# Attention projections on one core: the split weights of the first token half are kept in DRAM and read back for the second

## The chip, the core and the metric

The kernel runs on one core of a Trainium2 chip. A core has five engines with a queue of instructions each: TensorE (PE in the profile; its weight loads are shown apart as PEld), VectorE (DVE), ScalarE (ACT), GpSimd (POOL) and SyncE (SP), which in this kernel mostly issues DMA transfers. Engines run side by side and wait for each other by semaphores; transfers between DRAM and on-chip memory run on the core's 16 DMA engines. The metric is the time on the device in microseconds (us) of one execution, as the median over several.

## The reference

Two residual layers over 1024 tokens of width 1024, in float32, and a last RMSNorm. Layer 0 has a retention and RWKV-7 mixer; layer 1, which the change touches, has grouped-query attention over a window of 128 tokens with a learned sink per head. A SwiGLU FFN follows each.

```python
def swa_sink_mixer(h, w_qkv, b_qkv, sinks, w_o, b_o):
    z = h @ w_qkv + b_qkv
    q, k, v = jnp.split(z, [SWA_WIDTH, SWA_WIDTH + SWA_KV_HEADS * HEAD_DIM], axis=-1)
    ...
    s = jnp.einsum('bnqhgd,bnkhd->bnhgqk', q, kb).astype(jnp.float32) * HEAD_DIM ** -0.5
    s = jnp.where(valid[None, :, None, None], s, -jnp.inf)
    m = jnp.maximum(jnp.max(s, axis=-1, keepdims=True), sink)
    e = jnp.exp(s - m)
    p = e / (jnp.sum(e, axis=-1, keepdims=True) + jnp.exp(sink - m))
    o = jnp.einsum('bnhgqk,bnkhd->bnqhgd', p.astype(vb.dtype), vb)
    return o.reshape(B, T, SWA_WIDTH) @ w_o + b_o

def reference(x, ...):
    h = x
    for layer in range(DEPTH):
        n = rms_norm(h, norm1_g[layer])
        h = h + (retention_rwkv_mixer(n, ...) if layer % 2 == 0 else swa_sink_mixer(n, ...))
        n = rms_norm(h, norm2_g[layer])
        h = h + swiglu(n, ffn_w_gate[layer], ffn_w_up[layer], ffn_w_down[layer])
    return rms_norm(h, final_g)
```

w_qkv is 1024 x 1536 (16 query heads, 4 key heads and 4 value heads of 64), w_o is 1024 x 1024.

## The kernel before

Features lie on the 128 partitions and tokens along the free axis. The 1024 tokens are worked in two halves of 512 (`hf` 0 and 1), and each half runs through every weight, so each weight of the attention is loaded twice.

**Splitting.** Matrix products are made from operands split in two: a high part rounded to the type fp32r and a low part, which is what the rounding leaves. A product is three matmuls, high by high, high by low and low by high (`gemm`, L350 to L352). For a weight the split runs on the chip. `wraw` (L303) loads 128 columns of a weight, 128 x 1024 raw numbers or 512 KB, from DRAM through SP's queue (L305) into one of two buffers `wr`. `wsplit` (L327) cuts it into two tiles of 512 columns: for each, ACT casts the high part (L335) and an engine named by `self.lo` subtracts (L336) to give the low part. In the attention that engine is DVE. A split tile of 128 x 2 x 512 numbers is 512 KB. `wtile` (L317) hands out its place: in the attention and the FFN around it, from a ring of six, four under the tag `w` and two under `wx`. One weight is two tiles, and one `gemm` with it is 24 matmuls of 128 x 128 by 128 x 512.

**Keeping.** The mixer of layer 0 already stores its split weights in DRAM in token half 0 (`wsplit` with `keep`, L338) and reads them back in half 1 (`wkept`, L308, the transfer at L313, from a ring of four), under the name `wsp`.

**The attention.** `attn(hf)` makes 12 projections with `proj`: two tiles of keys, two of values, eight of queries; each loads a weight, runs a gemm and scales the result on DVE and on ACT. The keys are copied with halves exchanged to a second tile `ks` by two DMAs each on SP's queue (L1520, L1521). Then for each of four groups of heads, after its two query projections, four blocks of 128 queries: scores on PE (L1552), the mask added on DVE (L1556), the row maximum on DVE (L1562), the exponentials on ACT (L1569), the scaling by the sum on DVE (L1578) and for one head of four on ACT, transposes on PE (L1585), the product with the values on PE (L1595), and the split of the result (L1601 on ACT, L1602 on DVE). These are 16 blocks in each half, 32 in all. `w_o(hf)` then runs eight more weights over the result and adds it to the residual (L1613).

**The order.** In `trunk` the calls stand as: norm of half 0, two of the eight output tiles of the down projection of layer 0's FFN for half 1 (`rest_d`), `attn(0)`, the rest of those, norm of half 1, `w_o(0)`, `form0` (it forms the operands of the next FFN for half 0 and stores them in DRAM as `bd`, by eight DMAs at L1134), `attn(1)`, five pairs of the first part of the FFN of layer 1 (`early`), `w_o(1)`, and the rest of the FFN. That is only the order in which they are written down: when the kernel is built, a scheduler with a model of time fills each engine's queue from all of them, as far as buffers and data allow, so gemms of one part run between the softmax steps of another. On the chip each queue then runs in the order that was built.

Of the kernel before, what the change touches and what calls it, by code (L numbers as in the profile page):

```python
# [10 lines left out]
F32 = mybir.dt.float32  # L11
# [5 lines left out]
P = 128  # L17
T = 1024
HT = 512
# [85 lines left out]
class Plan:  # L105
# [3 lines left out]
    def __init__(self, K):  # L109
        self.K, self.now, self.ev, self.banks = K, 0.0, {}, []  # L110
        self.gens, self.jobs, self.cur, self.twice = [], deque(), None, ()
# [93 lines left out]
class Kern:  # L205
    def __init__(self, ctx, tc, A, out):
        self.ctx, self.tc, self.nc, self.A, self.out = ctx, tc, tc.nc, A, out
        nc = self.nc
        self.pp = ctx.enter_context(tc.tile_pool(name="pp", bufs=1, side="left"))
        self.dr = ctx.enter_context(tc.tile_pool(name="dr", bufs=2, space=bass.MemoryType.DRAM))  # L210
        self.n = 0
        pad = ctx.enter_context(tc.tile_pool(name="pad", bufs=1, side="right"))
        pt = pad.tile([P, 120], F32, tag="pad", name="pad")
        nc.gpsimd.memset(pt, 0.0)
        nc.scalar.activation(pt[:, :16], pt[:, :16], AF.Copy)
        self.gapt(self.pp, 32)
        self.pv = self.t(self.pp, [P, NPV], "pv")
        nc.scalar.dma_start(self.pv, A["pvec"])
        self.cst = {}
        for nm in ("ones", "eps"):  # L220
            self.cst[nm] = self.const(self.pp, nm)
        self.h, self.plan = [None, None], None
        self.wx = None
        self.w6, self.nw, self.owed, self.lo = False, 0, [], self.nc.gpsimd
        self.hid = [self.dram(f"hid{i}", [FT, P, HT]) for i in range(4)]
        self.hc = [self.dram(f"hc{L}", [NP, 4, P, 2, HT]) for L in range(2)]
        self.bd = self.dram("bd", [KT, P, HT])
        self.u0d = self.dram("u0", [NP, 2, P, HT])
        self.wsp = self.dr.tile([30, 2, P, 2, HT], F32, tag="wsp", name="wsp", bufs=1)
        self.cats = [self.dram(f"cat{hf}", [KT, P, HT]) for hf in range(2)]  # L230

    def psum(self, name, bufs):
# [109 lines left out]
    def wload(self, ap, width=1024):  # L342

        return self.wsplit(self.wraw(ap, width), width)

    def gemm(self, ps, w, rhs):
        nc = self.nc
        n = len(rhs)
        for k, ((hi, lo), (rh, rl)) in enumerate(zip(w, rhs)):
            nc.tensor.matmul(ps, hi, rh, start=k == 0, stop=False)  # L350
            nc.tensor.matmul(ps, hi, rl, start=False, stop=False)  # L351
            nc.tensor.matmul(ps, lo, rh, start=False, stop=k == n - 1)  # L352
# [1145 lines left out]
    def attn(self, hf, nr, ap, n8):  # L1498
# [4 lines left out]
        amask, sink, b8 = self.amask, self.sink, self.b8  # L1503

        def proj(ti, out, **kw):
            w = self.wload(self.A["w_qkv"][ti])
            ps = self.pst("f", [P, HT])
            self.gemm(ps, w, nT)
            V.tensor_tensor(out=out, in0=ps, in1=r, op=ALU.mult)
            S.activation(out, out, AF.Identity, **kw)  # L1510

        kc, ks = [], []
        for i in range(2):
            kt = self.t(ap, [P, P + HT], f"kc{i}", 2)
            proj(8 + i, kt[:, P:], bias=self.col("bqkv", 8 + i))
            st = self.t(ap, [P, P + HT], f"ks{i}", 1)
            lo = 0 if hf else P
            if hf:
                G.tensor_copy(kt[:, 0:P], self.pk[i][:, HT : HT + P])
            nc.sync.dma_start(st[0:64, lo:], kt[64:128, lo:])  # L1520
            nc.sync.dma_start(st[64:128, lo:], kt[0:64, lo:])  # L1521
            kc.append(kt)
            ks.append(st)
# [4 lines left out]
        for i, vc in enumerate(vcs):  # L1528
            proj(10 + i, vc, bias=self.col("bqkv", 10 + i))
# [8 lines left out]
        for g in range(4):  # L1538
            for i in (2 * g, 2 * g + 1):
                proj(i, qt[i], scale=0.125, bias=b8[:, i : i + 1])  # L1540
            for b in range(4):
                ti, rg = g // 2, g % 2
# [62 lines left out]
    def w_o(self, hf, ch):  # L1605
        nc = self.nc
        h = self.h[hf]
        for d in range(KT):
            w = self.wload(self.A["w_o"][d])
            ps = self.pst("f", [P, HT])  # L1610
            self.gemm(ps, w, ch)
            hk = self.kt(h)(d)
            nc.vector.scalar_tensor_tensor(  # L1613
                out=hk, in0=hk, scalar=self.col("bo", d), in1=ps, op0=ALU.add, op1=ALU.add
            )
# [225 lines left out]
```

## Time and profile before

| | us |
|---|---|
| three runs | 2384.56, 2380.51, 2376.88 |
| their median | 2380.51 |
| the profiled execution | 2374.81 |
| its span in the trace | 2373.0 |

In the profile, a row "L335 ACT CAST w<-wr" is an instruction of line 335 on ACT that reads `wr` and writes `w`. A matmul reads a moving operand and a weight (`ps_f<-n,w`). Half 0 of the attention runs in about 1310 to 1515 us of the trace, half 1 in about 1515 to 1760, each with parts of the neighbouring stages between. Matmuls overlap, so that one of 0.39 us may start 0.23 us after the one before.

### The profile page before, as it was taken

The numbers are of one execution on the slowest core, as the hardware profiler recorded it, in microseconds if no ns is written. First come the engines' busy times: TensorE is split into PE (matmuls) and PEld (weight loads), VectorE is DVE, ScalarE is ACT, GpSimd is POOL, SyncE is SP. The second block draws the span as 40 slices with busy tenths as digits, with TensorE's granted clock in tenths as the row PEclk, the third lists the DMA queues.
The fourth block names the chain that finished last, engine by engine and source line by source line (L and its number), as shares of the span: only waits on it lengthen the run. The fifth ranks groups of instructions, "written<-read, shape, count | busy, mean of one in ns | idle before, by whom it ended". The sixth has DMA issues, their size and how long they took to land. (4 is left out here: it accounts for less than half of the span.)

```text
span 2373.0 us, 35626 instructions
## 1 busy us (share of the span) xinstructions
PE 2312.1 (97%) x13092; PEld 1828.9 (77%) x13092; DVE 1667.4 (70%) x2630; ACT 1054.7 (44%) x1946; POOL 948.4 (40%) x746
## 2 busy tenths in 40 slices
PE   8999999999999999999999999999999999999997
PEld 6777777777777888888778877777787888877885
DVE  6876865774667358887675668567548778888776
ACT  5354533324456333333333556557645333333335
POOL 3123221201342057776667300002103577767665
PEclk9999999999999999999999999999999999999998
DMA  7555544443445545554554321232236465547652
GB/s 271 203 199 197 176 154 132 128 115 114 148 164 183 208 164 206 211 197 163 218 220 142 123 66 64 71 127 71 100 128 221 170 216 213 209 175 280 245 193 87
DMA packets 167741, 395.92 MB, mean 167 GB/s; under 512 B 42896, under 2 KB 45584, under 8 KB 167568
## 3 DMA queue, kind: packets, MB, share of 16 engines
q1 hardware_dynamic: 164448, 388.15, 47.8%
q10 hardware_dynamic: 2832, 4.45, 0.5%
q8 instruction: 104, 1.70, 0.3%
q0 software_dynamic: 288, 1.05, 0.1%
q14 instruction: 69, 0.57, 0.1%
HBM read 271.29 MB, written 116.92 MB: 164 GB/s over the span
## 5 line engine op out<-in xcount | busy, mean ns | idle before, releaser
L240 PE MATMUL ps_f<-n,w 128*128 128x512 f32 x1440 | 385.6, 415 | 8.6 <-ACT w L335 6.4
L240 PEld LDWEIGHTS ps_f<-n,w 128*128 128x128 f32 x1440 | 268.2, 192 | 93.6 <-issue 24.5
L335 ACT CAST w<-wr 128x512 fp32r<-128x512 f32 x244 | 147.9, 612 | 182.9 <-PE ps_f L352 73.1
L336 POOL TENSOR_TENSOR w<-wr,w 128x512 fp32r<-128x512 f32 x68 | 92.1, 1363 | 280.0 <-ACT w L335 223.0
L336 DVE TENSOR_TENSOR w<-wr,w 128x512 fp32r<-128x512 f32 (+1 forms) x176 | 123.8, 706 | 71.5 <-ACT w L335 71.3
L336 POOL TENSOR_TENSOR w<-wq,w 128x512 fp32r<-128x512 f32 x92 | 130.5, 1431 | 29.2 <-ACT w L335 27.2
L351 PE MATMUL ps_f<-n,w 128*128 128x512 f32 x356 | 141.7, 398 | 0.0
L352 PE MATMUL ps_f<-n,w 128*128 128x512 f32 x356 | 141.0, 396 | 0.6 <-POOL w L336 0.6
L350 PE MATMUL ps_f<-n,w 128*128 128x512 f32 x356 | 140.8, 396 | 0.6 <-ACT n L1601 0.5
L1182 DVE TENSOR_TENSOR nq<-ps_m,u 128x512 f32<-128x512 f32 x88 | 58.8, 685 | 104.3 <-PE ps_m L1177 104.2
L336 POOL TENSOR_TENSOR wx<-wr,wx 128x512 fp32r<-128x512 f32 x8 | 10.6, 1319 | 301.8 <-ACT wx L335 301.6
L1175 PE MATMUL ps_f<-n,w 128*128 128x512 f32 x298 | 118.5, 398 | 4.7 <-DVE h L1375 3.1
L1175 PE MATMUL ps_m<-n,w 128*128 128x512 f32 x300 | 117.5, 392 | 1.5 <-DVE h L1375 1.5
L1176 PE MATMUL ps_f<-n,w 128*128 128x512 f32 x298 | 117.2, 393 | 0.1
L1176 PE MATMUL ps_m<-n,w 128*128 128x512 f32 x300 | 116.8, 389 | 0.0
L1177 PE MATMUL ps_m<-n,w 128*128 128x512 f32 x300 | 116.8, 389 | 0.0
L1177 PE MATMUL ps_f<-n,w 128*128 128x512 f32 x298 | 116.7, 393 | 0.0
L358 POOL TENSOR_TENSOR n<-nq,n 128x512 fp32r<-128x512 f32 x54 | 91.5, 1707 | 8.9 <-ACT n L356 8.9
L1175 PE MATMUL ps_m<-cb,w 128*128 128x512 f32 x240 | 93.4, 389 | 1.0 <-DVE nq L1182 1.0
L1176 PE MATMUL ps_m<-cb,w 128*128 128x512 f32 x240 | 93.4, 389 | 0.0
L1177 PE MATMUL ps_m<-cb,w 128*128 128x512 f32 x240 | 93.4, 389 | 0.0
L1349 POOL TENSOR_TENSOR w<-wd,w 128x512 fp32r<-128x512 f32 (+1 forms) x53 | 76.0, 1444 | 34.8 <-ACT w L1348 34.8
(525 smaller groups left out, 6467.1 us busy)
## 6 DMA issues: line engine op xcount, KB each, us to landing
hc<-n SPq DMA_DIRECT2D x74, 512.0 KB, 2.6
wsp<-w SPq DMA_DIRECT2D x54, 512.0 KB, 3.3
w<-wsp SPq DMA_DIRECT2D x54, 512.0 KB, 3.4
wq<-in_w_gate SPq DMA_DIRECT2D x44, 512.0 KB, 4.3
u<-u SPq DMA_DIRECT2D x88, 256.0 KB, 2.9
n<-hc SPq DMA_DIRECT2D x43, 512.0 KB, 5.5
wr<-in_w_in SPq DMA_DIRECT2D x34, 512.0 KB, 4.8
hid<-n SPq DMA_DIRECT2D x66, 256.0 KB, 2.0
```

What stands on the lines that cost most here:

```text
L240: self.nc.tensor.matmul(out, lhsT, rhs, **kw)
L335: nc.scalar.copy(hi[:, :n], raw[:, c])
L336: self.lo.tensor_tensor(out=lo[:, :n], in0=raw[:, c], in1=hi.bitcast(F32)[:, :n], op=ALU.subtract)
L350: nc.tensor.matmul(ps, hi, rh, start=k == 0, stop=False)
L351: nc.tensor.matmul(ps, hi, rl, start=False, stop=False)
L352: nc.tensor.matmul(ps, lo, rh, start=False, stop=k == n - 1)
L358: e.tensor_tensor(out=lo, in0=src, in1=hi.bitcast(F32), op=ALU.subtract)
L1175: mm(ps, hi, xh, start=first and k == 0, stop=False, skip_group_check=True)
L1176: mm(ps, hi, xl, start=False, stop=False, skip_group_check=True)
L1177: mm(ps, lo, xh, start=False, stop=last and k == len(w) - 1, skip_group_check=True)
L1182: add = lambda o, x, y: V.tensor_tensor(out=o, in0=x, in1=y, op=ALU.add)
L1349: nc.gpsimd.tensor_tensor(out=lo, in0=v, in1=hi.bitcast(F32), op=ALU.subtract)
```

## The change

A tile `wsa` is added in DRAM for the 20 weights of the attention (12 of w_qkv, 8 of w_o), in two split tiles each. A new method `wtwice` takes the place of `wload` at both calls. In half 0 it loads and splits as before and stores each split tile to `wsa`; in half 1 it reads the two tiles back into the ring, and does not load the raw weight or split it. All of these transfers are on SP's queue. One line is added at L230 and eleven behind `wload`, so that the line numbers of the changed kernel are higher by 1 from there and by 12 from `gemm` on.

```diff
         self.wsp = self.dr.tile([30, 2, P, 2, HT], F32, tag="wsp", name="wsp", bufs=1)
+        self.wsa = self.dr.tile([20, 2, P, 2, HT], F32, tag="wsa", name="wsa", bufs=1)
...
+    def wtwice(self, ap, kept, again):
+
+        if not again:
+            return self.wsplit(self.wraw(ap), keep=kept)
+        res = []
+        for i in range(2):
+            w = self.wtile()
+            self.nc.sync.dma_start(w.bitcast(F32), kept[i])
+            res += [(w[:, 0, k * P : k * P + P], w[:, 1, k * P : k * P + P]) for k in range(4)]
+        return res
...
         def proj(ti, out, **kw):
-            w = self.wload(self.A["w_qkv"][ti])
+            w = self.wtwice(self.A["w_qkv"][ti], self.wsa[ti], hf)
...
         for d in range(KT):
-            w = self.wload(self.A["w_o"][d])
+            w = self.wtwice(self.A["w_o"][d], self.wsa[12 + d], hf)
```

## The prediction

> **What bounds the kernel now.** I read the busy shares first, then the waits of TensorE (PE) around the two attention layers, then the stretches in which the edited lines run. The first row is from the page, the rows under it from the table of stretches (its columns: stretch, length, then busy time and instruction count of PE, of its weight loads, of VectorE (DVE), ScalarE (ACT) and GpSimd (POOL), granted clock, DMA share, GB/s), and the last three from the list of PE's waits between 1300 and 1800 us (total, times, longest).
>
> ```profile
> PE 2312.1 (97%) x13092; PEld 1828.9 (77%) x13092; DVE 1667.4 (70%) x2630; ACT 1054.7 (44%) x1946; POOL 948.4 (40%) x746
> ```
>
> ```profile
> 1310.00:1515.00 205.00, 200.77 (x1014) 152.96 (x1013) 146.67 (x324) 121.92 (x307) 18.84 (x18) 1.00 0.23 75
> 1515.00:1760.00 245.00, 245.00 (x1198) 186.23 (x1197) 152.75 (x308) 138.07 (x320) 31.11 (x24) 1.00 0.30 99
> ```
>
> ```profile
> PE ps_y L1595 <- DVE n L1602: 2.1, 3, 0.9
> PE ps_m L1585 <- DVE s L1578: 1.7, 1, 1.7
> PE ps_f L350 <- ACT n L1601: 0.5, 1, 0.5
> ```
>
> Attention of token half 0 lies in the first stretch, that of half 1 in the second. In the second PE is busy 245.00 of 245.00 us at full clock, while DVE has 92 us and ACT 107 us free: nothing that those engines do holds PE up. All of PE's waits in the region are 4.3 us; that is 205.00 − 200.77 = 4.2 of the first stretch, so all lie in half 0, none in half 1. The two lines that split a weight, L335 and L336, release none of them.
>
> **The change part by part.** Half 1 loses 20 raw loads, 40 casts on ACT and 40 subtractions on DVE, and gains 40 reloads; half 0 gains 40 stores. The built order of each engine confirms it: ACT falls by 40 instructions, DVE by 40, SP rises by 60 DMA issues, and PE and POOL keep their counts.
>
> *Removed work.* The groups by line in 1515 to 1760 (count | busy, mean ns | idle time before, and what ended it):
>
> ```profile
> L335 ACT CAST w<-wr 128x512 fp32r<-128x512 f32 x46 | 28.4, 618 | 42.5 <-PE ps_f L352 36.7 <-PE ps_f L1177 5.1 <-DMA wr<-in_w_qkv 0.5
> L335 ACT CAST wx<-wr 128x512 fp32r<-128x512 f32 x22 | 13.7, 620 | 20.8 <-PE ps_f L352 18.2 <-DMA wr<-in_w_qkv 2.6
> L336 DVE TENSOR_TENSOR w<-wr,w 128x512 fp32r<-128x512 f32 x29 | 20.0, 689 | 20.3 <-ACT w L335 20.2
> ```
>
> 40 × 0.618 = 24.7 us go from ACT and 40 × 0.689 = 27.6 us from DVE. The casts stand waiting for PE (36.7 and 18.2 us for a gemm to free a tile), not PE for them. So the saving lands on engines that already wait for PE, in a stretch where PE has no idle time to give back: 0 us. Between the ends 0 and −27.6, PE's 245.00 of 245.00 says 0. The Trainium skill, page "Perfetto Trace Analysis", section "Identifying the Most-Contended Engine", holds that matmul busy time is a bad measure of how full TensorE is, because matmuls are pipelined, and that the busy share of weight loads is a good one: by it this term could be larger than 27.6 us, which is Rival C's second price.
>
> *Reloads in half 1.* A reload is one 512 KB transfer into one ring tile. It may start once PE has finished with the tile that held the slot, and must land before PE comes to it. PE in time order, where the ring of six runs with nothing between:
>
> ```profile
> 1517.05 0.39 PE L350 MATMUL ps_f<-n,wx 128*128 128x512 f32 x1
> ...
> 1519.77 0.39 PE L350 MATMUL ps_f<-n,wx 128*128 128x512 f32 x1
> ...
> 1533.37 0.39 PE L350 MATMUL ps_f<-n,wx 128*128 128x512 f32 x1
> ```
>
> The tile of 1517.05 is done with by 1519.77, 2.72 us for 12 matmuls, 0.227 us each; its slot's next content is first read at 1533.37. That is 13.6 us of lead, five tiles. The same store and reload exist for the mixer's weights; issues with KB and us to landing, then the issue times on SP's queue (min/median/max ns):
>
> ```profile
> wsp<-w SPq DMA_DIRECT2D x54, 512.0 KB, 3.3
> w<-wsp SPq DMA_DIRECT2D x54, 512.0 KB, 3.4
> ```
>
> ```profile
> L338 SPq DMA_DIRECT2D wsp<-w x54: 319/327/1496, 24.9 to 266.9; - x54
> L313 SPq DMA_DIRECT2D w<-wsp x54: 319/326/637, 302.8 to 580.7; - x54
> DMA to landing us min/median/max: 2.6/3.4/6.7
> ```
>
> A reload costs 0.33 + 3.4 = 3.7 us, so 9.9 us of the lead are spare, and 6.6 us in the worst landing (6.7). It needs 512 KB in 2.72 us, 193 GB/s. The mixer's reloads ran in 302.8 to 580.7, with a ring of four. The stretch around them, and PE's waits in it as listed (total, times, longest):
>
> ```profile
> 300.00:590.00 290.00, 283.96 (x2675) 216.43 (x2674) 182.43 (x428) 103.39 (x164) 49.37 (x72) 0.98 0.43 129
> ```
>
> ```profile
> PE ps_c L240 <- DVE TZ L870: 3.2, 4, 1.5
> PE ps_c L240 <- DVE GT L945: 1.8, 1, 1.8
> PE ps_m L240 <- DVE AR L933: 0.7, 1, 0.7
> ```
>
> No wait is for a reload: 54 of them cost PE nothing. I take 0 for these 40; the other end is Rival A's 21.6.
>
> *Stores in half 0.* 40 × 0.327 = 13.1 us more of issuing on SP. A store waits for the subtraction L336, and a raw load waits already for the L336 that frees its buffer, as SP's waits in 1300 to 1800 show:
>
> ```profile
> SPq L305 <- DVE w L336: 157.4, 30, 26.7
> SPq L1134 <- DVE u L1123: 5.0, 5, 3.2
> ```
>
> So the next raw load, queued behind the store, comes 0.33 to 0.65 us later and no more. What is new is the traffic: 512 KB read and 1 MB written per weight, in a dense gemm of 24 × 0.227 = 5.45 us, 289 GB/s. The nearest rows are the opening of the mixer, which reads and stores in the same way:
>
> ```profile
> 20.00:60.00 40.00, 39.18 (x166) 29.66 (x165) 23.23 (x34) 19.89 (x30) 15.65 (x24) 1.00 0.75 266
> ```
>
> ```profile
> wr<-in_w_in SPq DMA_DIRECT2D x12, 512.0 KB, 5.1
> ```
>
> ```profile
> wr<-in_w_qkv SPq DMA_DIRECT2D x12, 512.0 KB, 3.3
> ```
>
> There a raw load took 5.1 us to land instead of 3.3, and PE lost 0.82 us in 40. At that rate the 205 us of half 0 would lose 4.2 us. But a load that is 1.8 + 0.65 us later is covered by the ring's 13.6 us, of which cast and subtraction take 1.3. Ends 0 and +4.2; I take 0.
>
> *Sum.* Profiled run 2374.81 us (span 2373.0 plus 1.81 around it) − 0 + 0 + 0 = 2374.8. That run lies 5.7 below the median of the three, 2380.51, so on the basis of the median the sum is 2380.5.
>
> **The rivals.**
>
> *A, slower: reloads late on SP's queue.* SP issues in order. In half 1 the reloads share it with the copies of kc into ks (L1520, L1521) and the eight stores of u (L1134), which wait for DVE; SP in time order (start, length, then count):
>
> ```profile
> 1547.93 2.31 SPq L1134 DMA_DIRECT2D bd<-u  x4
> ...
> 1554.97 4.22 SPq L1134 DMA_DIRECT2D bd<-u  x4
> 1559.29 21.96 SPq L305 DMA_DIRECT2D wr<-in_w_qkv  x5
> ```
>
> In the changed order these stand among reloads nine to twelve and those behind them. A raw load was one step of two and ran a weight ahead; a reload cannot go before its slot is free. It decides once SP is held for longer than the spare 9.9 us. Then a tile is issued when it is needed: 3.7 us of waiting, and PE loses its clock. That second price is in this row, after the 3.10 us wait at its middle:
>
> ```profile
> 1219.00:1227.00 8.00, 6.24 (x20) 5.00 (x21) 6.38 (x9) 1.56 (x4) 3.02 (x3) 0.79 0.00 0
> ```
>
> ```profile
> 1220.76 0.47 PE L1175 MATMUL ps_f<-n,w 128*128 128x512 f32 x1 [3.10 <-DVE h L1375]
> ```
>
> (1 − 0.79) × 8 = 1.7 us. Four tiles: 4 × 5.4 = 21.6, so 2402.1. Against it: the longest wait of a store of u is 3.2 us, a third of what is spare, and all five sum to 5.0.
>
> *B, slower: softmax packed tighter.* With DVE and ACT relieved, the build puts the transposes of blocks 17 to 24 (of 32) nearer to their scores on PE: between them lie 10.4 to 16.2 us of other matmuls, where it was 11.4 to 19.9. The softmax in that time:
>
> ```profile
> L1556 DVE TENSOR_TENSOR s<-ps_r,c_amask 128x512 f32<-128x512 f32 x16 | 11.0, 685 | 4.3 <-PE ps_c L1552 3.5 <-PE ps_r L1552 0.9
> L1562 DVE TENSOR_REDUCE st<-s 128x4 f32<-128x1024 f32 x16 | 19.4, 1214 | 0.1
> L1569 ACT ACTIVATE s<-s,st 128x256 f32<-128x256 f32 x64 | 31.7, 497 | 1.2 <-DVE st L1566 1.2
> L1578 DVE TENSOR_SCALAR s<-s,st 128x256 f32<-128x256 f32 x48 | 16.7, 405 | 0.1
> ```
>
> 2 × 0.685 + 1.214 + 4 × 0.497 + 3 × 0.405 = 5.8 us at least, so 4.6 us are left at the tightest, while the work that used to slip in between (L336) is less. If that is used up, each of the eight blocks pays the one such wait seen, 1.7 us (L1585 behind L1578): +13.6, 2394.1.
>
> *C, faster: DVE was in the way after all.* If the 27.6 us off DVE reached the end, 2352.9. It needs PE to wait for DVE in half 1, and no row shows such a wait. A second price: PE's busy row hides waiting inside its overlapping matmuls, and only the weight loads are work, 186.23 of the 245.00; then up to 58.8 us could go, 2321.7. The page of the Trainium skill named above would have it so. Against it: matmuls of the dense run start every 0.227 us without a gap and a weight load takes 0.188 (this row), so that run too would be only 83% full by this measure, with nothing to wait for.
>
> ```profile
> L352 PEld LDWEIGHTS ps_f<-n,w 128*128 128x128 f32 x127 | 23.8, 188 | 5.8 <-issue 1.0
> ```
>
> *D, a little faster.* The 4.3 us of waits in half 0 go away in the new order: 2376.2, still no change by the bound below. DVE and ACT keep all their work in half 0, which speaks against it.
>
> **How the numbers follow.** No change within 0.3% (7.1 us, what a measurement here can tell, since three runs lie 7.7 apart) has 0.68: the forecast 0.62 and D 0.06. Faster has 0.09: C 0.04 (its second price 0.01 of it), and 0.05 for a new order that also saves waits outside the region, which I could not price. Slower has 0.23: A 0.12, B 0.08, and 0.03 for stores that cost twice their upper end. Forecast: 2380.5, with its own range of 2372 to 2389 (−4.3 and +4.2, and runs that scatter by 4). The whole range reaches past B's 2394.1 and half of A, 2380.5 + 2 × 5.4 = 2391.3, up to 2396; down to 2370.
>
> **What would show it.** Right: in half 1 ACT and DVE busy some 25 and 28 us less, PE still busy for all of its stretch, no wait of L350 to L352 for a DMA into a w or wx tile, and in half 0 no wait for L335. Wrong by A: waits of PE for w<-wsa of 2 us and more with a clock under 1.00 behind them. By B: more waits L1585 <- L1578. By the stores: raw loads landing in over 10 us, and ACT's L335 waiting for them. By C: a shorter half 1 with PE at the same number of matmuls, which would mean that its 245.00 us were not work.

## The result and the profile after

The changed kernel takes 2383.24 us (median of 11 runs, 2379.96 to 2392.18); the kernel before, in 11 runs, 2376.83 (2370.84 to 2384.56). The ratio is 1.0030 with a 95% interval of 1.0018 to 1.0042: slower by some 6 to 7 us, where no change was forecast. The profiled execution has a span of 2381.1 us.

The stages that the prediction worked on came out as it said. First the table of stretches of the kernel after, with the two of the attention:

```profile
1310.00:1515.00 205.00, 200.78 (x1003) 152.38 (x1002) 144.10 (x322) 119.74 (x303) 17.91 (x17) 0.98 0.44 157
1515.00:1760.00 245.00, 245.00 (x1192) 185.48 (x1191) 123.36 (x268) 113.61 (x278) 29.69 (x23) 1.00 0.47 157
```

In half 1 DVE is busy for 123.36 us where it was 152.75, and ACT for 113.61 where it was 138.07: 29.4 and 24.5 us less, against 27.6 and 24.7 worked out. PE is still busy 245.00 of 245.00, with 1192 recorded matmuls where it had 1198. Its waits between 1300 and 1800 us (total, times, longest) are the three of before, to the tenth:

```profile
PE ps_y L1607 <- DVE n L1614: 2.1, 3, 0.9
PE ps_m L1597 <- DVE s L1590: 1.7, 1, 1.7
PE ps_f L362 <- ACT n L1613: 0.5, 1, 0.5
```

None is for a reload. The rows of the stores and reloads, from the view of the tile in DRAM (issue time in ns, first and last start, then landing times of stores and reloads together), and two rows of who waited for the reused slots:

```profile
L339 SPq DMA_DIRECT2D wsa<-w x27: 319/320/1037, 1340.0 to 1522.7; - x27
L354 SPq DMA_DIRECT2D w<-wsa x27: 319/320/491, 1527.1 to 1746.8; - x27
...
  DVE wx L337: 3.4, 1
  ACT wx L336: 1.7, 2
...
DMA to landing us min/median/max: 2.5/3.9/6.6
```

The waits of DVE and ACT are in half 0: an engine that is to write a ring slot again must wait until the slot's store has been read out. The raw loads of half 0 land later, 5.5 us where they took 3.3 (the DMA view of 1310 to 1515 us):

```profile
wr<-in_w_qkv SPq DMA_DIRECT2D x12, 512.0 KB, 5.5
```

None of this reaches PE. To find where the time went, the same matmuls of the two executions were matched one by one, and the start before was taken from the start after:

```
time in the trace before (us)    1300   1450   1550   1750   1850   2200   2250   2350
later in the changed kernel      -1.0   -1.0   +1.7   +3.3   +1.8   +1.8   +8.0   +7.4
```

The steps at 1500 and between 1550 and 1850 are small. The second is given back by 1850. The first comes and goes with the execution: from the first scores to the end of the first addition of `w_o` it is 127.8 us in the kernel before, 130.3 here, 127.6 in e5 and 130.7 in e13, which has no edit there (e5 and e13 are experiments further down). It is the granted clock, the share of full speed at which PE's clock ran: over 1500 to 1515 us it is 1.00 in the kernel before and in e5, 0.89 here and 0.77 in e13. The step of 6.2 us is between 2200 and 2250, 450 us behind the last edited line: in the second down projection, the one of layer 1. Its stretches, kernel before and then kernel after:

```profile
2205.00:2215.00 10.00, 10.00 (x46) 8.28 (x45) 8.65 (x10) 1.95 (x4) 7.05 (x6) 1.00 1.03 416
2215.00:2225.00 10.00, 10.00 (x46) 8.29 (x45) 10.00 (x12) 6.13 (x11) 8.62 (x7) 1.00 0.11 39
```

```profile
2205.00:2215.00 10.00, 6.91 (x30) 5.09 (x28) 7.97 (x7) 1.86 (x3) 9.49 (x7) 1.00 1.02 410
2215.00:2225.00 10.00, 9.03 (x33) 7.29 (x34) 10.00 (x18) 3.45 (x6) 3.39 (x2) 0.83 0.43 170
```

PE stands for 3.1 and 1.0 us of these twenty and runs the second ten at a granted clock of 0.83, which is 1.7 us more. It waits for one line, here as the list of waits from 2190 to 2270 has it, and then as two rows of PE in time order:

```profile
PE ps_f L1187 <- DVE h L1387: 4.1, 2, 3.5
```

```profile
2206.73 0.47 PE L1187 MATMUL ps_f<-n,wr 128*128 128x512 f32 x1 [0.52 <-DVE h L1387]
...
2215.97 0.47 PE L1187 MATMUL ps_f<-n,w 128*128 128x512 f32 x1 [3.54 <-DVE h L1387]
```

L1187 is L1175 of before. In this stage one accumulator in PSUM serves two products: PE makes the first, DVE adds it into h (L1387, L1375 before), and only then may PE add the second to the same bank. DVE's queue holds besides the preparation of the next group's weights, sums of wd into ws. Its order, kernel before:

```profile
2202.51 1.28 DVE L1375 TENSOR_TENSOR h<-h,ps_f 128x512 f32<-128x512 f32 x2
2206.35 1.72 DVE L1375 TENSOR_TENSOR ws<-wd 128x512 f32<-128x512 f32 x1 [2.56 <-POOL w L1349]
2207.99 0.68 DVE L1375 TENSOR_TENSOR h<-h,ps_f 128x512 f32<-128x512 f32 x1
```

and kernel after:

```profile
2205.91 1.27 DVE L1387 TENSOR_TENSOR h<-h,ps_f 128x512 f32<-128x512 f32 x2
2209.11 1.07 DVE L1387 TENSOR_TENSOR ws<-wd 128x512 f32<-128x512 f32 x1 [1.92 <-DMA wd<-in_w_down]
2210.28 1.59 DVE L1387 TENSOR_TENSOR ws<-ws,wd 128x512 f32<-128x512 f32 x1
2211.80 1.76 DVE L1387 TENSOR_TENSOR wd<-wd,wd 128x512 f32<-128x512 f32 x1
2213.49 1.74 DVE L1387 TENSOR_TENSOR ws<-wd 128x512 f32<-128x512 f32 x1
2215.15 0.68 DVE L1387 TENSOR_TENSOR h<-h,ps_f 128x512 f32<-128x512 f32 x1
```

Two things changed. The first pair of additions starts 3.4 us later (2205.91 for 2202.51). Of this 1.8 us is the lag that the execution has here anyway; four splits of hr (L370, L358 before) stand ahead of the pair in both kernels, but in another order, with one addition that had come before them now among them. And four preparations instead of one stand before the third addition, the first of them waiting 1.92 us for its weights to land. The third addition comes at 2215.15 instead of 2207.99, and PE, in need of that bank from 2212.4 on, starts again at 2215.97. No line of this stage was edited. The scheduler that fills the queues when the kernel is built came to another order here.

### The profile page after: what moved, and what is told of

It is laid out like the page before. It is cut to its first block, busy times and chain, and to the rows that moved or that the text cites. A ratio compares the mean times of both kernels' runs of the same rounds, so it can differ in the third digit from the quotient of the medians.

```text
span 2381.1 us, 35647 instructions
## 1 busy us (share of the span) xinstructions
PE 2312.5 (97%) x13092; PEld 1826.3 (77%) x13092; DVE 1636.4 (69%) x2590; ACT 1030.3 (43%) x1906; POOL 948.7 (40%) x746
## 5 line engine op out<-in xcount | busy, mean ns | idle before, releaser
L336 ACT CAST w<-wr 128x512 fp32r<-128x512 f32 x217 | 131.1, 611 | 158.8 <-PE ps_f L364 42.4
L337 DVE TENSOR_TENSOR w<-wr,w 128x512 fp32r<-128x512 f32 (+1 forms) x149 | 105.4, 711 | 59.8 <-ACT w L336 59.5
L337 POOL TENSOR_TENSOR wx<-wr,wx 128x512 fp32r<-128x512 f32 x8 | 10.3, 1288 | 302.8 <-ACT wx L336 302.8
L1187 PE MATMUL ps_f<-n,w 128*128 128x512 f32 x298 | 118.5, 397 | 8.1 <-DVE h L1387 6.5
L1187 PE MATMUL ps_m<-n,w 128*128 128x512 f32 x300 | 117.6, 393 | 0.7 <-ACT w L1360 0.7
L370 POOL TENSOR_TENSOR n<-nq,n 128x512 fp32r<-128x512 f32 x54 | 91.5, 1706 | 8.9 <-ACT n L368 8.8
L1187 PE MATMUL ps_m<-cb,w 128*128 128x512 f32 x240 | 93.5, 390 | 0.9 <-DVE nq L1194 0.9
```

The lines of the kernel that those rows point to most:

```text
L336: nc.scalar.copy(hi[:, :n], raw[:, c])
L337: self.lo.tensor_tensor(out=lo[:, :n], in0=raw[:, c], in1=hi.bitcast(F32)[:, :n], op=ALU.subtract)
L370: e.tensor_tensor(out=lo, in0=src, in1=hi.bitcast(F32), op=ALU.subtract)
L1187: mm(ps, hi, xh, start=first and k == 0, stop=False, skip_group_check=True)
```

## The experiments

Theory *order*: the loss is the new order of the second down projection. Rival *traffic*: stores and reloads cost it on the shared queue and the DMA engines. Later a rival *half 1*: the reloads, or the softmax packed tighter, cost a part that the order leaves over. All were run beside the kernel before on the same chip. "down" is the time in the profiled execution from the first to the last copy of L1410 in the second down projection, "half 1" that from the end of the first addition of `w_o` (L1613) in half 0 to the start of this (both by the line numbers of the kernel before).

| | n | mean us | before | difference | ratio, 95% interval | half 1 | down |
|---|---|---|---|---|---|---|---|
| kernel before, profiled | | | | | | 633.0 | 160.7 |
| the change | 11 | 2383.9 | 2377.3 | +6.6 | 1.0030 (1.0018 to 1.0042) | 631.7 | 167.8 |
| e1 change, DVE pinned | 12 | 2380.0 | 2376.3 | +3.8 | 1.0012 (0.9998 to 1.0025) | 632.1 | 162.2 |
| e2 before, DVE reordered | 11 | 2376.8 | 2376.3 | +0.6 | 0.9999 (0.9988 to 1.0011) | 632.1 | 163.8 |
| e3 stores alone | 12 | 2376.5 | 2376.3 | +0.3 | 1.0002 (0.9991 to 1.0014) | 633.1 | 160.0 |
| e4 before, both pinned | 11 | 2371.1 | 2376.3 | -5.2 | 0.9973 (0.9963 to 0.9984) | 633.0 | 160.0 |
| e5 change, old order | 12 | 2377.1 | 2374.5 | +2.6 | 1.0008 (0.9997 to 1.0019) | 633.3 | 160.1 |
| e6 before, new order | 12 | 2379.0 | 2374.5 | +4.5 | 1.0017 (1.0004 to 1.0030) | 631.8 | 164.3 |
| e7 reloads alone | 6 | 2384.2 | 2374.5 | +9.7 | 1.0035 (1.0022 to 1.0048) | 631.8 | 166.8 |
| e8 change, both pinned | 12 | 2372.5 | 2374.5 | -2.0 | 0.9990 (0.9980 to 1.0000) | 631.9 | 161.8 |
| e9 the change again | 9 | 2382.2 | 2375.3 | +6.8 | 1.0026 (1.0015 to 1.0037) | 633.1 | 163.9 |
| e10 change, old order again | 11 | 2377.2 | 2375.3 | +1.8 | 1.0010 (1.0001 to 1.0019) | 633.2 | 160.0 |
| e11 w_o alone | 11 | 2377.2 | 2375.3 | +1.8 | 1.0007 (0.9996 to 1.0019) | 633.1 | 160.0 |
| e12 w_qkv alone | 5 | 2383.7 | 2375.3 | +8.3 | 1.0034 (1.0021 to 1.0048) | 633.2 | 162.2 |
| e13 before, both pinned again | 12 | 2370.2 | 2375.8 | -5.7 | 0.9974 (0.9963 to 0.9984) | 633.1 | 160.8 |
| e14 change, all pinned | 12 | 2373.3 | 2375.8 | -2.6 | 0.9991 (0.9980 to 1.0003) | 632.0 | 161.6 |
| e15 reloads doubled | 6 | 2386.2 | 2375.8 | +10.3 | 1.0048 (1.0034 to 1.0062) | 643.8 | 162.8 |

A mean here has an error of about 1 us (the runs of one kernel scatter by about 3.3), a difference one of 1 to 1.7.

**e1, DVE's queue put right in the changed kernel.** In `down`, the sums and differences `ws` that prepare the second group's weights are issued behind the last of the four additions:

```diff
-                op(h1(2 * dp + 1), h1(2 * dp + 1), A[dp])
+                hk = h1(2 * dp + 1)
+                last = self.nc.vector.tensor_tensor(out=hk, in0=hk, in1=A[dp], op=ALU.add)
...
-                s1.append(op(self.wsum(fp, n, 4, 8), a21, a22))
+                with self.tc.issue_after(last.ins) if L and gi == 1 else nullcontext():
+                    s1.append(op(self.wsum(fp, n, 4, 8), a21, a22))
```

> The change as it is, but in the last down stage VectorE's four preparations of the next group's weights (sums of wd into ws) are queued behind the four additions into h that free the accumulators. Every other engine's order is the one of the changed kernel. Theory order (the loss is VectorE's new order there: waits of 3.54 and 0.52 us of TensorE on L1387 and the slow clock behind the longer one, 6.2 us from 2200 to 2250 in the aligned traces): the loss goes, the time is that of the kernel before within 2 us, and no wait of TensorE on h is left near 2200 us. Theory traffic (stores and reloads on the shared queue and DMA engines cost the 6.4 us between the medians): nothing changes, still 6 us above the kernel before.

The waits near 2200 us went, but only about half of the loss with them: +3.8, with an interval from 0.5 us below the kernel before to 5.9 above. Neither theory alone.

**e2, the same queue put wrong in the kernel before.**

```diff
+                if L and gi == 1 and dp in (1, 2):
+                    self.tc.add_manual_dep(adds[dp + 1].ins, v.ins.name, ...)
```

> The kernel before, without any store or reload, with only VectorE's queue in the last down stage put into the order that the changed kernel has there (the third addition into h behind the second sum of the next group, the fourth behind the third). Theory order: slower than before by 4 to 7 us, with the two waits of TensorE on h near 2210 us. Theory traffic: the time of the kernel before within 2 us.

PE waits for h, but less than in the changed kernel: the row holds 2.9 us of the first down projection as well, which leaves 1.8 here by the list from 2150 to 2300 us.

```profile
PE ps_f L1175 <- DVE h L1457: 4.8, 2, 2.9
```

The stage is 3 us longer in this execution, but over the runs the time is that of before (+0.6, by the interval at most 2.6). The place of the third and fourth additions alone is not the whole loss. Traffic had the right number here.

**e3, the stores alone.** `wtwice` splits in both halves, and keeps in half 0.

```diff
-        if not again:
-            return self.wsplit(self.wraw(ap), keep=kept)
+        return self.wsplit(self.wraw(ap), keep=None if again else kept)
```

> Only the 40 stores of half 0 are added; half 1 loads and splits its weights as before, and nothing reads the stores. As built, the last down stage has the order of the kernel before on all engines. Theory order: 0 within 2 us. Theory traffic, if the stores carry the cost: slower by up to 6 us, with raw loads landing late in 1310 to 1515 us.

+0.3: the stores, the rival's larger part, cost nothing that can be measured, though they raise the traffic of half 0 to 163 GB/s from 75. That does away with traffic as the stores' work.

**e5, e6 and e10, the whole order exchanged.** The changed kernel built with the order of the kernel before in the second down projection on PE, DVE, ACT and POOL (SP's is the same in both), and the other way round. The instructions are named by their place from the end of the traced program, and `add_manual_dep` only fixes which of two comes first in a queue:

```diff
+        TAIL = {mybir.EngineType.Activation: [141, 136, 140, 139, 135, ...], ...}
+        for eng, ranks in TAIL.items():
+            done = [i for i in tc.nc.cur_bb.bb.instructions if i.engine == eng]
+            for x, y in zip(ranks, ranks[1:]):
+                tc.add_manual_dep(done[-y], done[-x].name, ...)
```

> The change in full, but in the last down stage PE, VectorE, ScalarE and GpSimd are all held to the order of the kernel before (some 20 instructions of an engine at most change places). Before this, VectorE's queue alone was put right in the changed kernel and recovered 3.8 of 7.6 us between the means, and VectorE's queue alone put wrong in the kernel before cost 0.6. Theory order, now of all four engines together: the time of the kernel before within 2 us. Theory half 1 (the reloads, or the tighter order of the softmax, cost what the first pin left over): 3 to 4 us above the kernel before.

> The kernel before, with no store and no reload, held in the last down stage to the order that the changed kernel has there on all four engines. Theory order: 5 to 8 us slower than before, with waits of TensorE on h near 2210 us of 3 us and more. Theory half 1: at most 4 us slower.

The stretch 2195 to 2260 us in e5 and then in e6:

```profile
2195.00:2260.00 65.00, 65.00 (x289) 53.83 (x288) 48.21 (x52) 23.30 (x41) 44.84 (x31) 1.00 0.67 244
```

```profile
2195.00:2260.00 65.00, 61.23 (x269) 50.08 (x268) 44.53 (x49) 20.59 (x35) 43.80 (x29) 1.00 0.63 227
```

With its old order the changed kernel has PE busy all of the stretch; with the new order the kernel before, which has neither a store nor a reload of these weights, waits 3.7 us in it and is 4.5 us slower, a little under the 5 to 8 expected. The order costs 4.5 us by e6 and 6.6 − 2.6 = 4.0 by e5; the two agree within their errors of 1 to 2 us. The part of it that e2 moved gave 0.6; which of the other moves matter was not tested. The clock behind such a wait isn't the same each time: over this stretch it is 1.00 in e6, but 0.97 in the changed kernel with its waits of 4.1 us in all.

> The change held to the order of the kernel before in the last down stage, a second time; the first gave 2.6 us above the kernel before, with an interval that holds zero. Theory order alone: within 2 us of the kernel before. Theory order and a smaller second cost: again 2 to 3 us above it, and the trace should then show where after 1300 us, since up to there the programs are the same.

> The change as it is, a second time, beside the next kernel on one chip. Its first measurement was 6.6 us above the kernel before (means). Theory order: 4 to 8 us, and 4 to 5 of it gone in the next kernel. Theory half 1: the same total.

On one chip, the change is 6.8 above the kernel before and the change in the old order 1.8: 5.0 from the order. The interval of e10 leaves out 1 by a hair, and e5 had +2.6, between what the two theories expected, so a rest of about 2 us looks real.

**e7, e11 and e12, parts of the change.** e7 reads back in half 1 from the mixer's `wsp` and stores nothing, so that half 1 multiplies by the mixer's weights; e11 and e12 use `wtwice` at one of the two calls only. The first two pairs of lines are e7's (its other call, for `w_o`, reads `wsp` too), then one line for e11 and one for e12, each of which has `wload` again at the call that is left out.

```diff
-            return self.wsplit(self.wraw(ap), keep=kept)
+            return self.wsplit(self.wraw(ap))
...
-            w = self.wtwice(self.A["w_qkv"][ti], self.wsa[ti], hf)
+            w = self.wtwice(self.A["w_qkv"][ti], self.wsp[ti], hf)
...
+            w = self.wload(self.A["w_qkv"][ti])
...
+            w = self.wload(self.A["w_o"][d])
```

> Half 1 reloads, but from the split weights of the mixer, so that half 0 has no stores; the second token half of the attention is computed with the wrong weights. As built, the last down stage has the order of the changed kernel on all engines. Theory order: as slow as the change, 5 to 8 us, all of it from 2200 to 2250 us. Theory half 1: as slow too, but with 3 to 4 us of it between 1515 and 1850 us in the aligned traces.

> Only the eight weights of w_o are stored and read back. As built, the last down stage has the order of the kernel before. Theory order: 0 within 2 us. A cost for each reload (3 us for 40): 1.2 us for these 16.

> Only the twelve weights of w_qkv are stored and read back. As built, the last down stage has the order of the changed kernel. Theory order: 4 to 5 us slower than before, with a wait of TensorE of 3 us and more on h near 2210 us. A cost for each reload alone (24 of 40): 2 us and no such wait.

As built, e7 and e12 have the new order of the second down projection, e3 and e11 the old. The times fall into the same two classes, 8 to 10 us above the kernel before against 0 to 2, and so does the column "down": 160.0 in both kernels of the one class, 162.2 and 166.8 in the other. What the scheduler does at 2200 us turns on whether w_qkv is reloaded 700 us earlier. The 9.7 and 8.3 us are more than the change's own 6.6 and 6.8 (few runs, 6 and 5) and more than was expected of either, and why is open; e12's wait near 2210 us is 1.8 us where 3 and more was expected. Half 1 as a cause has no support in the column: the kernels with reloads (e15 aside) have 631.7 to 633.3 us there and those without 631.8 to 633.1.

**e4, e8, e13 and e14, the pin of e1 in both down projections.** The first has the same wait, the 3.10 us at 1220 us that the prediction quoted for its clock. Without `L and`, the edit of e1 acts there too. e4 and e13 have it in the kernel before, e8 and e14 in the changed one; e14 also has the `TAIL` of e5 on PE, ACT and POOL, and on DVE up to the additions.

```diff
-                with self.tc.issue_after(last.ins) if L and gi == 1 else nullcontext():
+                with self.tc.issue_after(last.ins) if gi == 1 else nullcontext():
```

> The kernel before, with VectorE's preparations of the second group's weights queued behind the four additions in both down stages, the one of layer 0 near 1220 us too, where the kernel before has a wait of 3.10 us on h and a clock of 0.79 over 8 us. Theory order: that wait and its clock are the same thing at another place, 3.1 + 1.7 = 4.8 us faster than before. If the wait comes from something else (a late DMA, a slow addition), no change or a new wait beside it.

The stretch 1200 to 1240 us, kernel before and then e4:

```profile
1200.00:1240.00 40.00, 36.90 (x156) 30.03 (x156) 30.22 (x32) 12.81 (x22) 25.18 (x17) 0.96 0.57 210
```

```profile
1200.00:1240.00 40.00, 40.00 (x178) 33.11 (x178) 35.05 (x36) 16.05 (x27) 30.97 (x20) 1.00 0.67 239
```

The wait and the slow clock are gone and 5.2 us with them (5.7 in e13), for 4.8 worked out. This is the version that beats both kernels, at 0.9973.

> The change with VectorE's preparations of the second group's weights queued behind the four additions in both down stages; the same pins took 5.2 us off the kernel before (means). Theory order: 5 us faster than the kernel before. Theory half 1: 1 to 2 us faster than the kernel before.

e8 comes out at −2.0 us, the number of theory half 1, 3.2 short of e4. But all its engines other than DVE keep the new order of the second down projection. e14 takes that away, and e13 is e4 again on the same chip as e14.

> The kernel before with both down stages pinned, a second time, as the base for the next two on the same chip: 5 us faster than the kernel before, as the first time (5.2).

> The change with both down stages pinned, and ScalarE, GpSimd, PE and VectorE held to the order of the kernel before in the last one: from 2190 us on, every engine has exactly the order of e13. If the rest of 2 us belongs to the unstable wait at 1220 us, the two are equal within 1.5 us (both 5 us faster than before). If the reloads or the order of half 1 cost it, this one is 2 to 3 us slower than e13 (2 to 3 us faster than before).

e14 has exactly e13's order on every engine from 2190 us on, and no wait on h in either down projection. Still it is 3.1 us slower than e13, with an error of 1.5. That speaks for a second cost of the change and against the unstable wait at 1220 us as its source. The profiled executions of the two do not show where: "half 1" and "down" together are 793.6 us in e14 and 793.9 in e13. Matched one by one as above, e5 and e10 are 2.3 and 2.6 us behind the kernel before, and e14 is 2.6 behind e13, already at 1300 us, ahead of the first edited line; at the end of the span it is 2.4, 2.7 and 1.9. Up to 1250 us every engine runs the same order in both of each pair (one matmul at 528 us in e10 aside). And executions of one order differ at 1300 us by more than such a rest: the changed kernel is 1.0 us ahead of the kernel before there, e9 is 4.2 and e1 8.6 behind it. So one execution of each kernel can't find a rest of this size.

**e15, the reloads doubled,** in e14's kernel.

```diff
-            self.nc.sync.dma_start(w.bitcast(F32), kept[i])
+            for _ in range(2):
+                self.nc.sync.dma_start(w.bitcast(F32), kept[i])
```

> The kernel e14 with each of the 40 reloads issued twice in a row into the same tile; the down stages keep e14's order. If the reloads are as well hidden as forecast (a lead of 13.6 us for 3.7), a second landing still fits: equal to e14 within 1.5 us, no wait of TensorE on wsa. If each reload costs something that no wait shows, another 2 to 3 us; if the lead is short, waits for wsa appear.

Half 1 becomes 11.8 us longer, with waits that name the reload, from the list of 1300 to 1800 us:

```profile
PE ps_f L364 <- DMA w<-wsa: 3.2, 5, 1.2
```

This was not expected. The second transfer into a tile waits until the first has landed (5.6 us in the median of these reloads, 4.1 in the change), and SP's queue stands behind it: between 1500 and 1800 us SP waits 73 us for them. PE uses a tile in 2.72 us. The doubled traffic may add to this, since the DMA engines are busy for 0.97 of 1510 to 1560 us; the run doesn't part the two. So it doesn't measure the lead of one reload, but shows that late reloads cost what Rival A feared: 12.9 us above e14, though only 3.2 us stand in the wait that names them. In the change itself no such wait is seen.

## Why the prediction was wrong, point by point

- **Removed work, 0 us: right.** DVE and ACT lost 29.4 and 24.5 us, PE's stretch kept its 245.00, and "half 1" is 631.7 us where it was 633.0. Rival C with both prices is refuted. That goes for the rule of the Trainium skill too (page "Perfetto Trace Analysis", section "Identifying the Most-Contended Engine"): the weight loads' share of 76% did not mean room that this change could have used.
- **Reloads and stores, 0 us: right in every row, not shown to the last microsecond.** No wait of PE for a reload, none of PE for a raw load; the landing of 5.1 us borrowed from the mixer was 5.5. e3 bears out the stores. A rest of 2 to 3 us (e5, e10, e14) remains between the change and the kernel before when the order is the same. It is near the error of the differences, and no stage behind the first edited line holds it in a profiled execution. Its cause is open.
- **Rivals A, B and D: did not happen.** The waits for L1597 on L1590 are one of 1.7 us, as before, and the others of half 0 stayed too. Late reloads do cost time (e15), but A's condition wasn't met.
- **The sum: this step failed.** It priced the stretches in which edited lines run and carried the rest of the kernel over at zero: "PE and POOL keep their counts" was read as if it meant that they keep their order. The built orders differed at one place behind the attention, with some 20 instructions of an engine moved at most, and the text gave a new order elsewhere 0.05, as a gain that it could not price. It cost 4.0 to 5.0 us in e5, e6 and e10, three fifths to three quarters of the loss. The row for such a price stood in the prediction: the 3.10 us wait on h at 1220 us, with 1.7 us of clock, is the same mechanism at the same line, quoted there for its clock alone.
- **Range and sign.** 2383.24 lies inside the range and inside the forecast's own, 2372 to 2389. That is luck: the forecast stood on 2380.5 from three runs, 3.7 us above the median of eleven, 2376.83, and this covered over half of the loss. The interval of the ratio leaves out no change, and the slower side had 0.23, with mechanisms that had no part in it.

## What to carry to other kernels

Where a scheduler builds the queues, an edit has a second effect that the diff does not show: compare the built order on every engine over the whole program, and price each place that moved by the waits that the same code already has elsewhere in the profile. Work taken off engines that already waited for PE bought nothing here, and moving it to DMA was no gain by itself. A wait that shows up in such a comparison may be one that the old kernel has too: pinning the additions that free an accumulator ahead of the next group's preparation gave 5 us without any of the change.

## What the runs showed of the hardware that was not expected

The same sum on DVE takes 0.68 us or up to 1.80 when all its operands are in SBUF (`wd`, `ws`, `h`, `y`), and what differs is whether POOL was at work when it began. Kernel after, DVE in time order and then POOL:

```profile
2213.49 1.74 DVE L1387 TENSOR_TENSOR ws<-wd 128x512 f32<-128x512 f32 x1
...
2216.95 0.68 DVE L1387 TENSOR_TENSOR ws<-wd 128x512 f32<-128x512 f32 x1
...
2240.39 0.69 DVE L1387 TENSOR_TENSOR h<-h,y 128x512 f32<-128x512 f32 x1
...
2243.18 1.80 DVE L1387 TENSOR_TENSOR h<-h,y 128x512 f32<-128x512 f32 x1
```

```profile
2213.21 1.47 POOL L1361 TENSOR_TENSOR w<-wd,w 128x512 fp32r<-128x512 f32 x1 [0.20 <-ACT w L1360]
2221.61 1.39 POOL L1361 TENSOR_TENSOR w<-ws,w 128x512 fp32r<-128x512 f32 x1 [6.93 <-ACT w L1360]
...
2240.41 1.81 POOL L1361 TENSOR_TENSOR w<-wd,w 128x512 fp32r<-128x512 f32 x1 [0.91 <-ACT w L1360]
2243.13 1.29 POOL L1361 TENSOR_TENSOR w<-wd,w 128x512 fp32r<-128x512 f32 x1 [0.91 <-ACT w L1360]
```

The slow one of 2213.49 begins beside POOL's instruction of 2213.21; in the 6.9 us in which POOL has nothing to do, DVE's sums take 0.68. The last two of each list show that the order of starting decides: the sum of 2240.39 begins 0.02 us ahead of POOL and takes 0.69, while POOL's instruction takes 1.81; the one of 2243.18 begins 0.05 us behind POOL and takes 1.80, while POOL's takes 1.29. The additions that read PSUM are not slowed: those of 2205.91 take 1.27 us for two while POOL works (2203.69 to 2208.38). Each preparation that begins behind POOL delays the addition behind it by up to 1.1 us more. So the price of one order depends on how the two queues happen to lie to each other; that the new order waits for 3.5 us here in the changed kernel and in e9, and for 1.8 in e12, would fit this, but was not tested by itself.
